# Twenty sums of weights staged in DRAM by the mixer, and a fourth seven-product pair in each later gate-and-up block of the last feed-forward part

## The chip, the cores and the metric

The kernel runs on one core of a Trainium2 chip. It has five engines that work at once and meet at semaphores: TensorE (PE, matrix products), VectorE (DVE), ScalarE (ACT), GpSimd (POOL) and SyncE (SP, which here only starts transfers). DMA engines, 16 of them for the core, move data between DRAM and the core's memory. The metric is the device time of one execution, in microseconds (us); lower is better.

## The reference

One decoder layer on 256 tokens of width 2048, all in float32: x + 0.5 FFN1, then a mixer (sliding-window attention beside an RWKV-7 recurrence, both gated), then cross-attention into a memory of 256 rows, then x + 0.5 FFN2, then a norm. What the change touches is the second feed-forward part; the mixer and the cross-attention matter as the time in which something else can be prepared.

```
def swiglu(h, w_gate, w_up, w_down):
    return (jax.nn.silu(h @ w_gate) * (h @ w_up)) @ w_down

x = x + 0.5 * swiglu(rms_norm(x, ffn1_norm), ffn1_w_gate, ffn1_w_up, ffn1_w_down)
x = gated_parallel_mixer(x, ...)        # w_in, attention, RWKV-7, w_proj_attn, w_proj_rwkv, w_out
x = memory_cross_attention(x, mem, ...) # w_q, w_kv, w_o
x = x + 0.5 * swiglu(rms_norm(x, ffn2_norm), ffn2_w_gate, ffn2_w_up, ffn2_w_down)
return rms_norm(x, final_norm)
```

w_gate and w_up are 2048 x 5632, w_down is 5632 x 2048. All weights are read from DRAM once.

## The kernel before

**Products of two parts.** PE multiplies numbers of reduced precision here, so every float32 operand is split into a high and a low part, and one product is three matmuls (`times`, L412 high by high, L413 with the weight's low part, L414 with x's low part). A matmul takes 128 rows of a weight and 512 columns for 128 tokens.

**Items.** Weights come in items of two blocks of 128 rows by 512 columns (0.524 MB; 512 KB). `weight_plan` lists them in the order of use: FFN1 is items 0 to 139, the mixer and the cross-attention 140 to 379 (W_in up to 299, projR 300 to 315, W_out 316 to 347, the cross-attention's from 348), FFN2 from 380 on. Of gate and up, both weights of a column block are taken together: such an item is a pair, two blocks of rows of gate and two of up, and a column block of 512 is eight pairs, numbered 0 to 7. There are eleven column blocks; the first (j = 0) is taken weight by weight.

**Splitting.** `load` (L331) has SP fetch an item, single ones four ahead, in 0.524 MB or, in the feed-forward parts, 1.05 MB for two items of the same weight. `divide` splits it one or two items ahead of PE: ACT rounds the raw weight to its high part (`hi`, L339) and DVE subtracts to get the low part (`lo`, L340). Raw tiles have four buffers, high and low parts three. So the load four items on waits for the subtraction that frees its buffer, and ACT's rounding waits until PE is done with the item three back. SP issues its transfers in the order of the program: what waits at the head of its queue holds everything behind it. There are eight counters for SP's transfers, used in turn, so a transfer also waits for the one eight before it.

**Seven products for eight.** A pair needs eight products: two row blocks, gate and up, two halves of the tokens. `product_pair` does it with seven where `SEVEN` names the pair (0, 2 and 4): products of sums of x (`combinations`) with sums of the four weight blocks. For such a pair `divide` forms four sums of weights with DVE (L366 to L369, 128x512 each), two tiles of them, and splits these too (`two_parts`, `thi` on ACT at L347, `tlo` on DVE at L348; each of the four tiles `thia`, `tloa`, `thib`, `tlob` has one buffer). Of the up weight then only one block is split. A plain pair is 24 matmuls on PE, a seven-product pair 21.

**Order.** Side work (norms, attention, the recurrence's steps, the memory's preparation) is written as coroutines in groups; `Interleave.tick`, called twice an item by `product`, lets each group go on by a step. The order of every engine's instructions is fixed thereby when the program is built. The recurrence runs from 1107 to 1272 us of the span; its products alternate with items of W_in on PE, its masks are written by DVE (`mk`, L1186) and its operands are fetched by POOL (`xb`, `rb`, L1150 and L1152). POOL also fetches x (L1351) and the memory (L1343) for the cross-attention.

**Memory.** In the mixer, work tiles of 128x4x256 float32 come from one ring, `t4`, of `N4` = 20 buffers.

```
def two_parts(v, e):
    sp = at["pool"]
    hi = sp.tile([P, KU, 512], F32R, tag="thi" + e, name="thi")
    lo = sp.tile([P, KU, 512], F32R, tag="tlo" + e, name="tlo")
    act.copy(hi[:], v[:])
    dve.tensor_tensor(lo[:], v[:], f32(hi[:]), ALU.subtract)
    return hi, lo
```

Of the kernel before, what the change touches and what calls it, by code (L numbers as in the profile page):

```python
# [7 lines left out]
F32 = mybir.dt.float32  # L8
F32R = mybir.dt.float32r
AF = mybir.ActivationFunctionType  # L10
ALU = mybir.AluOpType
# [4 lines left out]
P = 128  # L16
# [3 lines left out]
KD = D // P  # L20
# [7 lines left out]
KU = 2  # L28
# [1 line left out]

UP, DOWN = 2.0**40, 2.0**-40
GROUPS = ((0, 4), (4, 4), (8, 3))
N4 = 20

AHEAD, LOADED = 2, 4


SEVEN, SEVEN_DOWN = (0, 2, 4), ((2, 4, 6), (2, 4))


class Act:
# [39 lines left out]
def feed_forward_plan(wg, wu, wd, last):  # L81
    for j0, nj in GROUPS:
        for j in range(j0, j0 + nj):
            if j == 0:
                for w in (wg, wu):
                    yield w, 0, KD, 0, 512
            else:
                yield (wg, wu), 0, KD, (j * 512, j * 512), SEVEN
        yield (wd, wd), 4 * j0, 4 * nj, (0, 512), SEVEN_DOWN[nj < 4]
        if last and (j0, nj) == GROUPS[-1]:  # L90
            for n in (2, 3):
                yield wd, 4 * j0, 4 * nj, n * 512, 512
        else:
            yield (wd, wd), 4 * j0, 4 * nj, (1024, 1536), SEVEN_DOWN[1]
# [38 lines left out]
def decoder_layer(ctx: ExitStack, tc: tile.TileContext, a: dict, out: bass.AP):  # L133
    nc = tc.nc
# [13 lines left out]
    bg.group("chain", 3)  # L148
    bg.group("norm", 1)
    bg.group("mem", 1)  # L150

    def f32(x):
        return x.bitcast(F32)
# [14 lines left out]
    def idle(n):  # L168
        for _ in range(n):
            yield  # L170
# [9 lines left out]
    def select(out, in_, pattern, op, fill, base, mult):  # L180
        pool.affine_select(
            out=out, in_=in_, pattern=pattern, compare_op=op, fill=fill, base=base,
            channel_multiplier=mult,
        )

    ident = cpool.tile([P, P], F32, name="ident")
    select(ident[:], ones[:], [[-1, P]], ALU.is_equal, 0.0, 0, 1)
    bdup = cpool.tile([P, 2, P], F32, name="bdup")[:, 0, :]
    center = cpool.tile([P, P], F32, name="center")

    def mixer_constants(sp):

        abias = sp.tile([P, 2, P], F32, name="abias")
        pool.memset(abias[:], 0.0)
        select(abias[:, 0, :], abias[:, 0, :], [[1, P]], ALU.is_gt, NEG, 0, -1)
        select(abias[:, 1, :], abias[:, 1, :], [[-1, P]], ALU.is_ge, NEG, 0, 1)

        ups = sp.tile([P, 2, P], F32, name="ups")[:, 0, :]
        pool.memset(ups, UP)
        mask3 = sp.tile([P, 3, P], F32, name="mask3")  # L200
        select(mask3[:, 0, :], ups, [[1, P]], ALU.is_gt, 0.0, 0, -1)
        select(mask3[:, 1, :], ups, [[1, P]], ALU.is_ge, 0.0, 0, -1)
        select(mask3[:, 2, :], ups, [[1, P]], ALU.is_ge, 0.0, 0, -1)

        mask_l = sp.tile([P, P], F32, name="mask_l")
        select(mask_l[:], ups, [[-1, P]], ALU.is_gt, 0.0, 0, 1)
        bdones = sp.tile([P, P], F32, name="bdones")
        bdmean = sp.tile([P, P], F32, name="bdmean")
        pool.memset(bdones[:], 0.0)
        pool.memset(bdmean[:], 0.0)  # L210
        pool.memset(bdup, 0.0)
        for e in range(2):
            q = slice(64 * e, 64 * e + 64)
            pool.memset(bdones[q, q], 1.0)
            pool.memset(bdmean[q, q], 1.0 / 64)
            pool.memset(bdup[q, q], UP)
        pool.tensor_tensor(center[:], ident[:], bdmean[:], ALU.subtract)
        keep = sp.tile([P, 2, P], F32, name="keep")
        pool.memset(keep[:], 1.0)
        pool.memset(keep[:, :, 0:1], 0.0)  # L220
        return abias, mask3, mask_l, bdones, bdmean, keep

    sinks = cpool.tile([P, 16], F32, name="sinks")

# [69 lines left out]

    plan, units, items, ends = [], [], [], []
    for entry in weight_plan(a):
        if entry is None:
            ends.append(len(units))  # L300
            continue
        plan.append(entry)
        w, k0, nk, c0, n = entry
        if not isinstance(w, tuple):
            for k in range(k0, k0 + nk, KU):
                items.append(((len(units),), False))
                units.append((w, k, c0, n))
            continue
        for k in range(k0, k0 + nk, 2 * KU):
            u = len(units)  # L310
            units += [(v, k + i, c, 512) for v, c in zip(w, c0) for i in (0, KU)]
            items += [((u + i, u + 2 + i), (k - k0) // KU + i in n) for i in range(2)]
    raws, parts = {}, {}
    at = {"item": 0, "product": 0, "pool": None}

    def load(u, pieces=None):

        if u >= len(units) or u in raws:
            return
        w, k, c0, n = units[u]  # L320
        wide = at["pool"] is not None and (u < ends[0] or u >= ends[1] + LOADED)
        m = 2 if wide else 1
        if wide:
            raw = at["pool"].tile([P, m * KU, n], F32, tag="raw2", name="raw2", bufs=4)
        else:
            raw = wp.tile([P, KU, n], F32, tag="raw", name="raw", bufs=4)
        for i in range(m):
            raws[u + i] = raw[:, i * KU : (i + 1) * KU, :]
        for i, queue in pieces or ((slice(0, m * KU), nc.sync),):
            rows = slice((k + i.start) * P, (k + i.stop) * P)  # L330
            queue.dma_start(raw[:, i], w[rows, c0 : c0 + n].rearrange("(a p) n -> p a n", p=P))  # L331

    def split_unit(u, rows=slice(0, KU)):
        n, raw = units[u][3], raws[u]
# [16 lines left out]
    def divide(i):  # L351


        if i >= len(items) or i in parts:
            return
        which, seven = items[i]
        if len(which) == 1:
            parts[i] = split_unit(*which)
            return
        g, u = which  # L360
        if not seven:
            parts[i] = split_unit(g), split_unit(u)
            return
        rg, ru = raws[g], raws[u]
        t = [wp.tile([P, KU, 512], F32, tag="raw", name="raw", bufs=4) for _ in range(2)]
        dve.tensor_tensor(t[1][:, 0], ru[:, 0], rg[:, 0], ALU.subtract)  # L366
        dve.tensor_tensor(t[0][:, 0], ru[:, 1], ru[:, 0], ALU.subtract)
        dve.tensor_tensor(t[0][:, 1], ru[:, 1], t[1][:, 0], ALU.subtract)  # L368
        dve.tensor_tensor(t[1][:, 1], rg[:, 1], t[0][:, 1], ALU.subtract)  # L369
        a_ = two_parts(t[0], "a")  # L370
        parts[i] = split_unit(g), split_unit(u, slice(1, 2)), (a_, two_parts(t[1], "b"))

    def next_item():
        i = at["item"]
        at["item"] += 1
        u = items[i][0][0]
        for v in range(u, u + (2 * LOADED if at["pool"] is not None else LOADED)):
            load(v)
        divide(i)
        room = AHEAD  # L380
        for j in range(i + 1, min(i + 1 + AHEAD, len(items))):
            room -= len(items[j][0])
            if room < 0:
                break
            for v in items[j][0]:
                load(v)
            divide(j)
        return parts[i]

    def product(x: Act, w, skew=False):  # L390
# [30 lines left out]
                k + i == 0, k + i == nk - 1,  # L421
            )

    def combinations(sp, x: Act, seven, name, ready=lambda: True, early=True):

        pairs = [q for q in range(max(seven) + 1) if early or q in seven]
        n = 12 if not early else sum(4 if q in seven else 2 for q in pairs)
        parts = [sp.tile([P, n, P], F32R, tag=name + e, name=name + e) for e in ("hi", "lo")]  # L430
        c = {"parts": parts, "at": {}, "done": False, "seven": seven, "early": early}

# [220 lines left out]
    def feed_forward(sp, x, norm: Norm, wg, wu, wd, done, begin_last=lambda: None, last=False):  # L653
        if last:
# [6 lines left out]
                sp.tile(shape, dt, tag=tag, name=tag, bufs=bufs)  # L661
        begun = at["item"]
        c = combinations(
            sp, norm.x, SEVEN, "c", lambda: norm.r is not None and at["item"] > begun + 4
        )
        c["next"] = []
        for gi, (j0, nj) in enumerate(GROUPS):
# [1 line left out]
                [sp.tile([P, 16, T], F32R, tag="hhi", name="hhi")],  # L669
                [sp.tile([P, 16, T], F32R, tag="hlo", name="hlo")], 16,  # L670
            )
            ch = combinations(sp, h, SEVEN_DOWN[nj < 4], "d", early=False)

            def transposed(hb, c):
                for q in range(2):
# [90 lines left out]

    with tc.tile_pool(name="mx", bufs=1, reuse_waits="tile") as sp:
        aligned(sp)
        abias, mask3, mask_l, bdones, bdmean, keep = mixer_constants(sp)

        def t4(name, shape=(P, 4, T), dt=F32):
            return sp.tile(list(shape), dt, tag="t4", name=name, bufs=N4)

        def act_tiles(name, n):
            return Act(
# [386 lines left out]
        def pair(h, j):  # L1162
# [12 lines left out]
            for c in range(2):  # L1175
# [34 lines left out]
                def stage(lhs, rhs, o, first, name):  # L1210
                    for e, r in enumerate(rows):
                        pe.matmul(  # L1212
                            vb[:, o : o + P][:, r], lhs(e), rhs[:, r],
                            start=first and e == 0, stop=True, **ek,
                        )
                    s = small(name)
                    act.copy(s[:], vb[:, o : o + P])
                    return s
# [27 lines left out]
                if c == 0:  # L1246
                    s0 = small("s0")
                    dve.scalar_tensor_tensor(
                        s0[:], bs, dec[h][:, j : j + 1], bdup, ALU.mult, ALU.mult
                    )  # L1250
                yield
            bg.seen.add(f"y{4 * h + j}")
# [260 lines left out]
```

## Time and profile before

| | |
|---|---|
| time, median of 3 runs | 2262.58 us (2262.24 to 2262.78) |
| the profiled execution | 2263.34 us, of it 2261.6 in the span |
| TensorE's granted clock | 0.999 |
| busy: PE, DVE, ACT, POOL | 2246.8, 1778.4, 1226.9, 132.2 us |
| matmuls | 10617 records |
| moved by DMA | 432.49 MB, of it 13.11 MB written to DRAM; mean 191 GB/s |
| DVE, the four sums of a pair (L366 and the three after it), 128x512 | 687 ns each |
| ACT high part, 128x1024 and 128x512 | 1051 and 620 ns |
| DVE low part, 128x1024 and 128x512 | 1231 and 686 ns |
| ACT `thi`, DVE `tlo`, 172 of each | 1050 and 1220 ns |
| stages of the span | FFN1 to about 640 us, mixer and cross-attention to about 1560, FFN2 to the end |

A row of a stretch gives its length and the busy time of each engine with the count of instructions, then TensorE's clock as a share of full speed, the mean busy share of the 16 DMA engines (waiting transfers can make it pass 1) and the rate in GB/s. A timeline row gives start, duration, engine, line, operation, the tiles written and read, and in brackets the idle time before it with what ended it. Durations of PE's matmuls overlap; their starts do not. A row of the transfers gives the tile, the issuing queue, the count, the size and the time from issue to landing.

### The profile page before, as it was taken

To read this page: it belongs to the slowest core of one execution; us is meant where nothing else is said; L and a number is where in the kernel's file an instruction comes from. 1 tells how busy PE (TensorE), PEld (TensorE's weight loads), DVE (VectorE), ACT (ScalarE), POOL (GpSimd) and SP (SyncE) were. 2 spreads that over 40 slices of the span, in tenths; PEclk is the share of its full clock that TensorE was granted. 3 is DMA by queue.
4 is the path that set the end of the run, shared out by engine and by line. 5 is a ranking of instruction groups with operands and counts; after the bars stand their busy time and mean duration, and the time that the engine had idled before them with its cause. 6 is when DMAs were issued, how large, how long until landed. Compare 5 with 4: busy or idle time off the path is not lost.

```text
span 2261.6 us, 28110 instructions
## 1 busy us (share of the span) xinstructions
PE 2246.8 (99%) x10617; PEld 1845.5 (82%) x10617; DVE 1778.4 (79%) x2281; ACT 1226.9 (54%) x1653; POOL 132.2 (6%) x192
## 2 busy tenths in 40 slices
PE   9999999999999999999999999999999999999998
PEld 7888888888888877788888888888888888888886
DVE  7899989998988477886434566547899988998987
ACT  6555555555556477444435446456555455555554
POOL 1000000000001000301220030001000000000002
PEclk9999999999999999999999999999999999999999
DMA  7555565555556544666433476647555565555564
GB/s 262 186 206 199 190 210 199 186 204 205 189 200 200 161 135 155 216 214 208 147 90 100 143 257 218 203 166 271 187 203 201 191 211 198 186 205 205 186 209 145
DMA packets 219144, 432.49 MB, mean 191 GB/s; under 512 B 14108, under 2 KB 16385, under 8 KB 219009
## 3 DMA queue, kind: packets, MB, share of 16 engines
q1 hardware_dynamic: 210432, 404.78, 52.7%
q0 software_dynamic: 8112, 25.12, 3.5%
q8 instruction: 83, 1.36, 0.2%
q10 hardware_dynamic: 464, 0.79, 0.1%
q14 instruction: 53, 0.43, 0.1%
HBM read 417.56 MB, written 13.11 MB: 190 GB/s over the span
## 4 chain that ended last, share of the span: by engine, by line
PE 96%; DVE 2%; issue 1%; DMA 1%; ACT 1%; SPq 0%; POOL 0%; POOLq 0%; DVEq 0%; ACTq 0%
PE acc L412 19%; PE acc L413 19%; PE acc L414 19%; PE mm L414 8%; PE mm L412 8%; PE mm L413 8%; PE tr L600 2%; PE tr L413 2%; PE tr L412 2%; PE tr L414 2%; PE mm L1212 1%; PE tr L1181 1%; DVE lo L340 1%; DMA raw<-in_w_out_dram 0%; PE mm L827 0%
## 5 line engine op out<-in xcount | busy, mean ns | idle before, releaser
L340 DVE TENSOR_TENSOR lo<-raw,hi 128x1024 fp32r<-128x1024 f32 (+1 forms) x770 | 894.0, 1163 | 352.9 <-ACT hi L339 351.2
L339 ACT CAST hi<-raw 128x1024 fp32r<-128x1024 f32 (+1 forms) x770 | 759.7, 997 | 747.5 <-PE acc L414 528.5
L412 PE MATMUL acc<-hi,xhi 128*128 128x512 f32 (+1 forms) x1196 | 477.7, 400 | 2.1 <-ACT xhi L627 1.7
L413 PE MATMUL acc<-lo,xhi 128*128 128x512 f32 (+1 forms) x1196 | 465.7, 389 | 0.0
L414 PE MATMUL acc<-hi,xlo 128*128 128x512 f32 (+1 forms) x1196 | 465.0, 389 | 0.0
L412 PEld LDWEIGHTS acc<-hi,xhi 128*128 128x128 f32 x1196 | 225.3, 188 | 52.1 <-issue 5.5
L413 PEld LDWEIGHTS acc<-lo,xhi 128*128 128x128 f32 x1196 | 225.2, 188 | 45.8 <-issue 3.2
L414 PEld LDWEIGHTS acc<-hi,xlo 128*128 128x128 f32 x1196 | 224.6, 188 | 46.5 <-DVE xlo L628 1.0
L347 ACT CAST thi<-raw 128x1024 fp32r<-128x1024 f32 x172 | 178.9, 1050 | 57.6 <-DVE raw L368 44.2
L348 DVE TENSOR_TENSOR tlo<-raw,thi 128x1024 fp32r<-128x1024 f32 x172 | 208.3, 1220 | 0.7 <-ACT thi L347 0.4
L412 PE MATMUL mm<-hi,xhi 128*128 128x512 f32 x380 | 149.5, 393 | 0.0
L414 PE MATMUL mm<-hi,xlo 128*128 128x512 f32 x380 | 148.3, 390 | 0.0
L413 PE MATMUL mm<-lo,xhi 128*128 128x512 f32 x380 | 148.3, 390 | 0.0
L413 PE MATMUL acc<-lo,hhi 128*128 128x512 f32 x372 | 145.7, 392 | 0.8 <-DVE lo L340 0.8
L414 PE MATMUL acc<-hi,hlo 128*128 128x512 f32 x372 | 145.7, 392 | 0.0
L412 PE MATMUL acc<-hi,hhi 128*128 128x512 f32 x372 | 145.1, 390 | 0.0
L414 PEld LDWEIGHTS mm<-hi,xlo 128*128 128x128 f32 x380 | 71.4, 188 | 15.0
L413 PEld LDWEIGHTS mm<-lo,xhi 128*128 128x128 f32 x380 | 71.4, 188 | 14.4
L412 PEld LDWEIGHTS mm<-hi,xhi 128*128 128x128 f32 x380 | 71.5, 188 | 14.4
L413 PEld LDWEIGHTS acc<-lo,hhi 128*128 128x128 f32 x372 | 69.9, 188 | 15.4 <-DVE lo L340 1.2
L412 PEld LDWEIGHTS acc<-hi,hhi 128*128 128x128 f32 x372 | 69.9, 188 | 14.3
L414 PEld LDWEIGHTS acc<-hi,hlo 128*128 128x128 f32 x372 | 70.0, 188 | 13.9
(384 smaller groups left out, 3550.2 us busy)
## 6 DMA issues: line engine op xcount, KB each, us to landing
raw<-in_ffn_w_up_dram SPq DMA_DIRECT2D x88, 1024.0 KB, 5.3
raw<-in_ffn_w_down_dram SPq DMA_DIRECT2D x88, 1024.0 KB, 5.1
raw<-in_ffn_w_gate_dram SPq DMA_DIRECT2D x84, 1024.0 KB, 5.1
raw<-in_w_in_dram SPq DMA_DIRECT2D x136, 512.0 KB, 3.5
raw<-in_w_out_dram SPq DMA_DIRECT2D x32, 512.0 KB, 4.4
raw<-in_w_proj_attn_dram SPq DMA_DIRECT2D x16, 512.0 KB, 3.8
raw<-in_w_proj_rwkv_dram SPq DMA_DIRECT2D x16, 512.0 KB, 5.9
raw<-in_w_cross_kv_dram SPq DMA_DIRECT2D x16, 512.0 KB, 3.7
```

What stands on the lines that cost most here:

```text
L339: at["hi"] = act.copy(hi[:, s], raw[:, s])
L340: at["lo"] = dve.tensor_tensor(lo[:, s], raw[:, s], f32(hi[:, s]), ALU.subtract)
L347: act.copy(hi[:], v[:])
L348: dve.tensor_tensor(lo[:], v[:], f32(hi[:]), ALU.subtract)
L412: pe.matmul(o, xh, hi, start=first, stop=False, **how)
L413: pe.matmul(o, xh, lo, start=False, stop=False, **how)
L414: pe.matmul(o, xl, hi, start=False, stop=last, **how)
L600: pe.transpose(b[:, o : o + P], tok[:, t, col : col + P], ident[:])
L1181: pe.matmul(b[e][:, m * P : (m + 1) * P], x1[r, j, cs_], x2[r, j, cs_], start=True, stop=True,)
L1212: pe.matmul(vb[:, o : o + P][:, r], lhs(e), rhs[:, r], start=first and e == 0, stop=True, **ek,)
```

## The change

In FFN2, pairs 0, 1, 2 and 4 of each of the ten later column blocks take seven products (`SEVEN_2`), where 0, 2 and 4 did; FFN1 is as before. For pairs 1 and 2 (`STAGED`), 20 in all, the four sums of weights are not formed when the pair is reached. Twenty coroutines of a new last group do that during the mixer: each waits for an item (`STAGE_AT`: 253, 255 ... 271, then 310, 315 ... 355), has SP load the pair's gate and up blocks (two transfers of 0.524 MB) into two `t4` tiles, lets four ticks pass, forms the sums on DVE in two steps of two subtractions, each placed behind the latest low part, lets eight ticks pass and has SP store both tiles to a DRAM tensor `sums` (two transfers of 0.524 MB).

In FFN2, `load_sums` has SP fetch a pair's two tiles of sums into the ring of raw tiles, an item ahead, and `divide` takes these. The block of up rows that such a pair no longer uses (the sums hold it) is left out of the load of up; where pairs 1 and 2 lie in different loads of two, a load is cut in two pieces or shortened.

`combinations` of x makes the four sums for pair 1 too, so its tiles have 18 slots in FFN2. For the staging tiles the ring `t4` has 22 buffers; two constants, `bdup` and `center`, move from the constant pool into the mixer's.

By count of the built instructions: PE 30 matmuls fewer; ACT 20 roundings more; DVE 80 subtractions more in the mixer and in FFN2 40 subtractions fewer, 20 low parts more and three operations on x more; SP 130 transfers more (40 loads and 40 stores in the mixer, 40 loads of sums and 10 pieces more in FFN2).

```diff
-N4 = 20
+N4 = 22
...
 SEVEN, SEVEN_DOWN = (0, 2, 4), ((2, 4, 6), (2, 4))
+SEVEN_2, STAGED = (0, 1, 2, 4), (1, 2)
+
+
+STAGE_AT = [*range(253, 277, 2)][:10] + [*range(310, 370, 5)][:10]
...
-                yield (wg, wu), 0, KD, (j * 512, j * 512), SEVEN
+                yield (wg, wu), 0, KD, (j * 512, j * 512), SEVEN_2 if last else SEVEN
...
     bg.group("mem", 1)
+    bg.group("stage", 4)
...
-    bdup = cpool.tile([P, 2, P], F32, name="bdup")[:, 0, :]
-    center = cpool.tile([P, P], F32, name="center")
+    cpool.tile([P, P], F32, name="shift")
...
+        bdup = sp.tile([P, P], F32, name="bdup")
+        center = sp.tile([P, P], F32, name="center")
...
-            items += [((u + i, u + 2 + i), (k - k0) // KU + i in n) for i in range(2)]
-    raws, parts = {}, {}
+            for i in range(2):
+                q = (k - k0) // KU + i
+                if n == SEVEN_2 and q in STAGED:
+                    staged[len(items)] = len(staged)
+                items.append(((u + i, u + 2 + i), q in n))
+    raws, parts, summed = {}, {}, {}
+    first_unused = {items[i][0][1] for i in staged}
+    sums_d = dram.tile([len(staged), P, 4, 512], F32, name="sums")
...
+        if u in first_unused:
+            second = u + 1 in first_unused
+            pieces = [(slice(1, 2), nc.sync)] + [(slice(2 + second, 4), nc.sync)]
+            if not second:
+                pieces = ((slice(1, 4), nc.sync),)
+        elif u + 1 in first_unused and wide:
+            pieces = ((slice(0, 2), nc.sync), (slice(3, 4), nc.sync))
         for i, queue in pieces or ((slice(0, m * KU), nc.sync),):
             rows = slice((k + i.start) * P, (k + i.stop) * P)
             queue.dma_start(raw[:, i], w[rows, c0 : c0 + n].rearrange("(a p) n -> p a n", p=P))
+
+    def load_sums(i):
+
+        if i not in staged or i in summed:
+            return
+        summed[i] = [
+            wp.tile([P, KU, 512], F32, tag="raw", name="raw", bufs=4) for _ in range(2)
+        ]
+        for e, t in enumerate(summed[i]):
+            nc.sync.dma_start(t[:], sums_d[staged[i], :, KU * e : KU * e + KU, :])
+
+    def stage(t4, i, n):
+
+
+        while at["item"] < STAGE_AT[n]:
+            yield
+        t = t4("su", (P, KU, 512)), t4("sg", (P, KU, 512))
+        for e, v in zip(t, items[i][0][::-1]):
+            w, k, c0, _ = units[v]
+            rows = slice(k * P, (k + KU) * P)
+            nc.sync.dma_start(e[:], w[rows, c0 : c0 + 512].rearrange("(a p) n -> p a n", p=P))
+        yield from idle(4)
+        u0, u1, g0, g1 = (e[:, c] for e in t for c in range(KU))
+        with tc.issue_after(at["lo"].ins):
+            dve.tensor_tensor(g0, u0, g0, ALU.subtract)
+            dve.tensor_tensor(u0, u1, u0, ALU.subtract)
+        yield
+        with tc.issue_after(at["lo"].ins):
+            dve.tensor_tensor(u1, u1, g0, ALU.subtract)
+            dve.tensor_tensor(g1, g1, u1, ALU.subtract)
+        yield from idle(8)
+        for c, e in enumerate(t):
+            nc.sync.dma_start(sums_d[n, :, KU * c : KU * c + KU, :], e[:])
...
-        rg, ru = raws[g], raws[u]
-        t = [wp.tile([P, KU, 512], F32, tag="raw", name="raw", bufs=4) for _ in range(2)]
-        dve.tensor_tensor(t[1][:, 0], ru[:, 0], rg[:, 0], ALU.subtract)
-        dve.tensor_tensor(t[0][:, 0], ru[:, 1], ru[:, 0], ALU.subtract)
-        dve.tensor_tensor(t[0][:, 1], ru[:, 1], t[1][:, 0], ALU.subtract)
-        dve.tensor_tensor(t[1][:, 1], rg[:, 1], t[0][:, 1], ALU.subtract)
+        t = summed.get(i)
+        if t is None:
+            rg, ru = raws[g], raws[u]
+            t = [wp.tile([P, KU, 512], F32, tag="raw", name="raw", bufs=4) for _ in range(2)]
+            dve.tensor_tensor(t[1][:, 0], ru[:, 0], rg[:, 0], ALU.subtract)
...
             for v in items[j][0]:
                 load(v)
+            load_sums(j)
             divide(j)
+        load_sums(i + 2)
         return parts[i]
...
         c = combinations(
-            sp, norm.x, SEVEN, "c", lambda: norm.r is not None and at["item"] > begun + 4
+            sp, norm.x, SEVEN_2 if last else SEVEN, "c", lambda: norm.r is not None and at["item"] > begun + 4
         )
...
-            ch = combinations(sp, h, SEVEN_DOWN[nj < 4], "d", early=False)
+            ch = combinations(sp, h, SEVEN_DOWN[nj < 4], "d", early=False, n=12)
...
+        for i, n in staged.items():
+            bg.spawn("stage", stage(t4, i, n))
```

More of the change, by code (lines that the diff above doesn't have):

```diff
@@ L210, in mixer_constants @@
         pool.memset(bdmean[:], 0.0)
-        pool.memset(bdup, 0.0)
+        pool.memset(bdup[:], 0.0)
         for e in range(2):
@@ L220, in mixer_constants @@
         pool.memset(keep[:, :, 0:1], 0.0)
-        return abias, mask3, mask_l, bdones, bdmean, keep
+        return abias, mask3, mask_l, bdup, center, bdones, bdmean, keep
     sinks = cpool.tile([P, 16], F32, name="sinks")
@@ L292, in decoder_layer @@
     junk_t = cpool.tile([P, 512], mybir.dt.bfloat16, name="junk")
-    plan, units, items, ends = [], [], [], []
+    plan, units, items, ends, staged = [], [], [], [], {}
     for entry in weight_plan(a):
@@ L363, in divide @@
             return
-        rg, ru = raws[g], raws[u]
-        t = [wp.tile([P, KU, 512], F32, tag="raw", name="raw", bufs=4) for _ in range(2)]
-        dve.tensor_tensor(t[1][:, 0], ru[:, 0], rg[:, 0], ALU.subtract)
-        dve.tensor_tensor(t[0][:, 0], ru[:, 1], ru[:, 0], ALU.subtract)
-        dve.tensor_tensor(t[0][:, 1], ru[:, 1], t[1][:, 0], ALU.subtract)
-        dve.tensor_tensor(t[1][:, 1], rg[:, 1], t[0][:, 1], ALU.subtract)
+        t = summed.get(i)
[3 more added lines that the diff above has]
+            dve.tensor_tensor(t[1][:, 0], ru[:, 0], rg[:, 0], ALU.subtract)
+            dve.tensor_tensor(t[0][:, 0], ru[:, 1], ru[:, 0], ALU.subtract)
+            dve.tensor_tensor(t[0][:, 1], ru[:, 1], t[1][:, 0], ALU.subtract)
+            dve.tensor_tensor(t[1][:, 1], rg[:, 1], t[0][:, 1], ALU.subtract)
         a_ = two_parts(t[0], "a")
@@ L422, in multiply, with combinations @@
             )
-    def combinations(sp, x: Act, seven, name, ready=lambda: True, early=True):
+    def combinations(sp, x: Act, seven, name, ready=lambda: True, early=True, n=0):
         pairs = [q for q in range(max(seven) + 1) if early or q in seven]
-        n = 12 if not early else sum(4 if q in seven else 2 for q in pairs)
+        n = n or sum(4 if q in seven else 2 for q in pairs)
         parts = [sp.tile([P, n, P], F32R, tag=name + e, name=name + e) for e in ("hi", "lo")]
@@ L768, in decoder_layer @@
         aligned(sp)
-        abias, mask3, mask_l, bdones, bdmean, keep = mixer_constants(sp)
+        abias, mask3, mask_l, bdup, center, bdones, bdmean, keep = mixer_constants(sp)
         def t4(name, shape=(P, 4, T), dt=F32):
             return sp.tile(list(shape), dt, tag="t4", name=name, bufs=N4)
+        for i, n in staged.items():
+            bg.spawn("stage", stage(t4, i, n))
         def act_tiles(name, n):
@@ L1248, in pair @@
                     dve.scalar_tensor_tensor(
-                        s0[:], bs, dec[h][:, j : j + 1], bdup, ALU.mult, ALU.mult
+                        s0[:], bs, dec[h][:, j : j + 1], bdup[:], ALU.mult, ALU.mult
                     )
```

## The prediction

> **What bounds the kernel now.** I read the page's busy shares and chain first, then issue intervals in the timeline, then stretches of the span with their transfer rate, then waits and transfer latencies where the change adds work.
>
> ```profile
> span 2261.6 us, 28110 instructions
> PE 2246.8 (99%) x10617; PEld 1845.5 (82%) x10617; DVE 1778.4 (79%) x2281; ACT 1226.9 (54%) x1653; POOL 132.2 (6%) x192
> PE 96%; DVE 2%; issue 1%; DMA 1%; ACT 1%; SPq 0%; POOL 0%; POOLq 0%; DVEq 0%; ACTq 0%
> ```
>
> PE is idle for 14.8 us of the span: a matmul less is time won, and whatever makes PE wait is time lost. The row duration of a matmul (0.39 us) overlaps its neighbours; the price is the issue interval. PE's timeline, start then duration:
>
> ```profile
> 699.70 0.39 PE L412 MATMUL acc<-hi,hhi 128*128 128x512 f32 x1
> ...
> 704.46 0.39 PE L412 MATMUL acc<-hi,hhi 128*128 128x512 f32 x1
> ```
>
> 21 intervals lie between these starts: 4.76/21 = 0.2267 us each.
>
> Stretches: us, then busy PE, PEld, DVE, ACT, POOL, the clock, the DMA share, GB/s. First late FFN2 (lines 1 and 2), then where sums are to be staged, then the highest rate.
>
> ```profile
> 1800.00:1850.00 50.00, 50.00 (x222) 41.46 (x221) 44.26 (x53) 26.58 (x30) 0.00 (x0) 1.00 0.59 207
> 2000.00:2050.00 50.00, 50.00 (x222) 41.45 (x221) 47.26 (x59) 26.33 (x28) 0.00 (x0) 1.00 0.60 210
> 1080.00:1100.00 20.00, 20.00 (x100) 16.49 (x99) 12.41 (x17) 9.83 (x12) 8.48 (x12) 1.00 0.55 171
> 1335.00:1434.00 99.00, 98.73 (x472) 81.17 (x471) 62.85 (x79) 56.70 (x95) 13.43 (x13) 1.00 0.67 227
> 1357.00:1360.00 3.00, 3.00 (x17) 2.50 (x16) 1.56 (x2) 1.64 (x2) 1.48 (x3) 1.00 0.95 229
> 1369.00:1372.00 3.00, 3.00 (x15) 2.46 (x15) 0.27 (x2) 1.05 (x1) 0.00 (x0) 1.00 1.03 375
> 1550.00:1555.00 5.00, 5.00 (x27) 4.12 (x26) 3.81 (x6) 4.30 (x10) 1.45 (x2) 1.00 1.05 406
> ```
>
> FFN2 is PE's alone, with DVE close behind. From 1357 to 1372 us the DMA engines are full already. Why, and what it does to a weight load, is in the issues (KB, us to landing; stretches 1351 to 1354 and 1359 to 1362), POOL's timeline, and ACT's (a bracket is idle time and releaser):
>
> ```profile
> raw<-in_w_out_dram SPq DMA_DIRECT2D x1, 512.0 KB, 3.5
> raw<-in_w_out_dram SPq DMA_DIRECT2D x1, 512.0 KB, 11.0
> 1355.59 0.72 POOL L1351 DMA_DIRECT2D x<-x1d  x1
> 1356.31 2.17 POOL L1343 DMA_DIRECT2D mem<-in_mem_dram  x3
> 1361.33 0.72 POOL L1343 DMA_DIRECT2D mem<-in_mem_dram  x1 [2.85 <-PE tr L600]
> 1370.65 1.05 ACT L339 CAST hi<-raw 128x1024 fp32r<-128x1024 f32 x1 [2.91 <-DMA raw<-in_w_out_dram]
> 1374.45 1.05 ACT L339 CAST hi<-raw 128x1024 fp32r<-128x1024 f32 x1 [0.66 <-PE acc L414]
> ```
>
> Five POOL loads of 0.524 MB meet the loads of W_out; a load that took 3.5 us takes 11.0. The cast at 1370.65 is of item 324 (W_out's ninth). Its low part ends at 1372.97; PE begins the item when ACT may write the cast two items on, at 1374.45. So 1.5 us of cushion is left, and PE lost nothing.
>
> **The change, part by part.**
>
> *Fewer products.* Ten blocks of the last FFN have a fourth pair with seven products for eight: per block 3 matmuls fewer, 30 in all, each 128x512. 30 x 0.2267 = 6.8 us, in a stretch with no PE idle. All of it counts.
>
> *Splitting in FFN2.* Per block (41.5 us of PE before, 40.8 after) two pairs read staged sums. DVE is 44.26/50 to 47.26/50 busy, 36.7 to 39.2 us a block. The sums of pairs 0, 2 and 4 were 12 subtractions of 0.687; now only pairs 0 and 4 make them, 8 (-2.7); the fourth pair adds two low parts of 1.22 (+2.4) and halves one of 1.23 to 0.69 (-0.5): 35.9 to 38.4. ACT, 22 us, adds two casts of 1.05 and halves one to 0.62 (+1.7). Both stay under PE's 40.8. DMA: 2.1 MB of sums more and 0.5 MB of unused rows less per block, about 207 to 250 GB/s against 406. Free in sum. In order it is tighter: pairs 0, 1, 2 now follow each other and share one buffer each for the parts of their sums, and a subtraction for pair 4, which waits for a load, stands on DVE ahead of pair 2's last low part (slack about 0.4 us by the order of the rows). Before, such subtractions waited 9 times for 8.6 us in FFN2. Ends: below nothing (DVE has 0.8 us a block less) by perhaps 0.3, and 0.5 us in each of ten blocks, 5. I take 0.6: two blocks of ten (9 waits in 42) at 0.3 each.
>
> *Staging, first ten (items 253 to 275, 1063 to 1170 us).* Each adds 2.75 us to DVE (4 x 0.687) and 2.1 MB: two loads, two stores, all on SP between the weight loads. From the first of them to the load of item 266 stand 28 transfers of 0.524 MB, 14.7 MB in 41 us: 355 GB/s, where 171 to 185 ran. At the 385 that the full stretches keep, the loads land in time; at 350 my queue count has item 266 2.5 to 3 us late. DVE is 39 to 44 of 45 us full up to 1107, and in the recurrence subtractions stand ahead of masks (L1186) for which PE waits already (twice, 0.2 us). POOL's loads of the recurrence's operands wait for earlier stores, with some 6 us to spare. Ends 0 and 3 (no gain: nothing is removed here); I take 0.8, nearer to the 385.
>
> *Staging, second ten (items 310 to 358, 1324 to 1480 us).* 2.1 MB per five items (13.6 us) is 154 GB/s on top of 227: 381. Between bursts the backlog clears. In the burst at 1357 it does not: ahead of item 324's load SP now issues both stores of the 12th sum and both loads of the 13th, 2.1 MB at 385 = 5.4 us. One of POOL's memory loads goes out of the burst, since it now waits for a store of the 14th sum: -1.4; cushion -1.5. That leaves 2.5. The first store also waits on SP for its subtractions with item 323's load behind it (up to 2 us, part of it hidden), and the burst's own mean was 315 GB/s, by which 2.1 MB take 6.7. I take 3.3. [...] The memory load that now goes late has 5 to 9 us before PE transposes it; x's loads queued behind it on POOL have as much.
>
> [...]
>
> *Constants moved, one more buffer pair, x's combinations in 18 slots for 16.* No instruction on PE; DVE and ACT gain 3 and one wider operation in FFN2's first block, under 2 us beside 40.8 of PE. Nothing.
>
> **Sum.** -6.8 + 0.6 + 0.8 + 3.3 = -2.1. The profiled execution took 2263.34 (span 2261.6 and 1.7 around it), so 2261.2; it lies 0.76 above the median 2262.58, from which the forecast is 2260.5.
>
> **The rivals.**
> 1. *The transfers are absorbed.* For: 406 GB/s at 1550, 385 over 9 us of the burst, no PE loss before. Against: 1.5 us of cushion. With 0 to 2.3 us given back in all: 2255.8 to 2258.1, named 2257.
> 2. *Staged traffic is slower than weight loads, and PE waits (slower).* Place: the second ten. The trace has hardly any writes (13 of 432 MB) and the burst with mixed transfers averaged 315 GB/s. From item 307's load to the last store 54.5 MB go in 153 us, 356 GB/s; at 315 they take 173, 20 late, less some 10 of load-ahead: 10, and 3 in the first ten. 2262.6 - 6.8 + 13.6 = 2269.4. It decides once all waits pass 11.3 us (about 325 GB/s).
> 3. *Three seven-product pairs in a row make PE wait in every block of FFN2.* 0.3 to 0.5 us x 10 for the 0.6 above: 2263 to 2265, named 2263.5. For: one buffer per part; against: DVE and ACT keep 2.4 and 17 us a block to spare.
>
> **How the numbers follow.** 0.2% is 4.5 us, about what a measurement of this kernel tells from no change. Forecast (give-back 2.3 to 7) 0.36, of which 0.02 under -0.2%; rival 1 0.29; rival 2 0.23, of which 0.21 over +0.2%; rival 3 0.12, of which 0.03 over. Faster 0.31, same 0.45, slower 0.24. The range: from 2255.8 (all hidden) to 2269 (rival 2's middle), leaving out about 0.04 below and 0.12 above. The likeliest case alone: 2258.1 to 2262.8.
>
> **What will show it.** PE's matmuls 30 fewer and FFN2 6 to 7 us shorter with no wait over 1 us: first step right; waits of PE on tlo or lo (L413's kind) in FFN2: rival 3. Between 1360 and 1380 casts waiting for W_out's loads by 5 us and more, PE idle 2 to 5 us: the second ten as forecast; none: rival 1; PE idle in several stretches from 1340 to 1480: rival 2. The first ten: PE's wait around item 266 and on the masks. The forecast is wrong if the rate of loads and stores together differs much from 385, or if the recurrence's chain suffers more than the 0.8.

## The result, and the profile after

The changed kernel takes 2267.04 us (median of 12 runs, 2265.0 to 2269.73), the kernel before 2262.36 (12 runs, 2262.13 to 2262.79): a ratio of 1.0021, 95% interval 1.0013 to 1.0028. It is slower by 4.7 us, 0.2%. Its runs scatter over 4.7 us where those of before lie within 0.7. The profiled execution took 2266.5 us, 2264.8 of it in the span, 3.2 more than before (whose profiled execution was 1.0 above its median).

The page of the changed kernel: span, busy engines, and a row of transfers (last number: us from issue to landing).

```profile
span 2264.8 us, 28418 instructions
PE 2242.4 (99%) x10587; PEld 1837.5 (81%) x10587; DVE 1825.7 (81%) x2344; ACT 1246.7 (55%) x1673; POOL 132.9 (6%) x192
raw<-in_w_out_dram SPq DMA_DIRECT2D x32, 512.0 KB, 7.0
```

The 30 matmuls are gone (10617 records to 10587) and PE is busy for 4.4 us less, yet idle for 7.6 us more (22.4 for 14.8). W_out's loads take 7.0 us, where they took 4.4.

Where it happens can be read off item by item. ACT casts every item's high part, two items ahead of PE, so the start of item k's cast after, less that of before, is how late PE's work is at that place, as long as the cast stands at the same place in ACT's order in both. From the timelines of ACT in the two profiled executions (us late):

| item | 256 | 274 | 313 | 319 | 328 | 341 | 356 | 383 |
|---|---|---|---|---|---|---|---|---|
| late | 0.0 | 0.8 | 0.5 | 0.9 | 6.7 | 8.6 | 10.2 | 10.2 |

The first ten sums cost 0.5 us and the second ten 9.7: 0.4 up to item 319, 5.8 in the burst up to 328, 1.9 around item 334, 1.6 around 348. FFN2 then gains: PE's last matmul starts at 2255.95 us for 2252.71, 3.2 late, so 7.0 us are won back there. That is the whole of the 6.8 forecast.

Stretches of the changed kernel (length, busy PE, PEld, DVE, ACT, POOL, clock, DMA share, GB/s):

```profile
1340.00:1440.00 100.00, 94.69 (x438) 76.24 (x437) 73.19 (x99) 52.76 (x88) 13.30 (x13) 0.98 0.91 318
1370.00:1375.00 5.00, 4.24 (x19) 3.13 (x18) 2.60 (x3) 1.05 (x1) 0.00 (x0) 1.00 1.04 404
1375.00:1380.00 5.00, 3.17 (x12) 1.75 (x10) 3.43 (x5) 3.14 (x3) 0.00 (x0) 1.00 1.05 388
1380.00:1385.00 5.00, 3.83 (x12) 2.97 (x13) 3.54 (x6) 0.95 (x2) 0.00 (x0) 0.66 1.02 371
```

PE loses 5.3 of the 100 us from 1340 on, 3.8 of them from 1370 to 1385, while the DMA engines move 371 to 404 GB/s. So the transfers are not slow; whose come first is what counts, and that the queue's order decides. That is in the timelines of SP and of DVE and ACT of the changed kernel, from the burst (start, duration, engine and line; in brackets the idle time before and what ended it):

```profile
1350.64 4.90 SPq L351 DMA_DIRECT2D raw<-in_w_out_dram  x3
1360.29 0.34 SPq L384 DMA_DIRECT2D sums<-su  x1
1361.42 0.37 SPq L351 DMA_DIRECT2D raw<-in_w_out_dram  x1
1361.89 0.51 SPq L372 DMA_DIRECT2D su<-in_ffn_w_up_dram  x1
1362.57 0.44 SPq L372 DMA_DIRECT2D sg<-in_ffn_w_gate_dram  x1
1363.12 0.51 SPq L384 DMA_DIRECT2D sums<-sg  x1
```

```profile
1358.12 0.69 DVE L376 TENSOR_TENSOR sg<-su,sg 128x512 f32<-128x512 f32 x1 [2.97 <-DMA sg<-in_ffn_w_gate_dram]
1359.57 0.69 DVE L380 TENSOR_TENSOR su<-su,sg 128x512 f32<-128x512 f32 x1
1371.09 1.05 ACT L392 CAST hi<-raw 128x1024 fp32r<-128x1024 f32 x1 [5.57 <-DMA raw<-in_w_out_dram]
1376.20 1.04 ACT L392 CAST hi<-raw 128x1024 fp32r<-128x1024 f32 x1 [4.06 <-DMA raw<-in_w_out_dram]
```

Read it backwards. The cast at 1371.09 is of item 323, and it waits for its load. That load goes out at 1361.42; before it went at 1356.80. Ahead of it in SP's queue stands the store of the 12th sum, which waits until 1360.29 for the third subtraction (1359.57 to 1360.26). The subtractions stand idle on DVE for 2.97 us because the sum's own raw weights land only at 1358.1. Behind item 323's load go three more staged transfers, and then item 324's load. So one late transfer of staged data passes to DVE's queue, from there to SP's, and from there to PE.

Of the kernel before, the loads of W_out that SP issues between 1355 and 1375 us, item 323's first (count, ns of an issue, first and last start):

```profile
L331 SPq DMA_DIRECT2D raw<-in_w_out_dram x6: 367/368/368, 1356.8 to 1373.0; - x6
```

### The profile page after: what moved, and what is told of

The parts are those of the page before. It is cut to its first block, busy times and chain, and to the rows that moved or that the text cites. A ratio compares the mean times of both kernels' runs of the same rounds, so it can differ in the third digit from the quotient of the medians.

```text
span 2264.8 us, 28418 instructions
## 1 busy us (share of the span) xinstructions
PE 2242.4 (99%) x10587; PEld 1837.5 (81%) x10587; DVE 1825.7 (81%) x2344; ACT 1246.7 (55%) x1673; POOL 132.9 (6%) x192
## 4 chain that ended last, share of the span: by engine, by line
PE 92%; DVE 3%; DMA 2%; issue 1%; ACT 1%; SPq 0%; POOL 0%; POOLq 0%; ACTq 0%; DVEq 0%
PE acc L469 18%; PE acc L471 18%; PE acc L470 18%; PE mm L471 8%; PE mm L470 8%; PE mm L469 8%; PE tr L657 2%; PE tr L470 2%; PE tr L469 2%; PE tr L471 2%; DMA raw<-in_w_out_dram 1%; DVE lo L393 1%; PE mm L1272 1%; PE tr L1241 1%; ACT hi L392 0%
## 5 line engine op out<-in xcount | busy, mean ns | idle before, releaser
L469 PE MATMUL acc<-hi,xhi 128*128 128x512 f32 (+1 forms) x1166 | 465.6, 400 | 2.7 <-ACT xhi L684 2.2
L470 PE MATMUL acc<-lo,xhi 128*128 128x512 f32 (+1 forms) x1166 | 453.4, 389 | 0.0
L471 PE MATMUL acc<-hi,xlo 128*128 128x512 f32 (+1 forms) x1166 | 453.3, 389 | 0.0
L469 PEld LDWEIGHTS acc<-hi,xhi 128*128 128x128 f32 x1166 | 219.4, 188 | 51.1 <-issue 5.4
L471 PEld LDWEIGHTS acc<-hi,xlo 128*128 128x128 f32 x1166 | 218.8, 188 | 45.8 <-DVE xlo L685 1.0
L470 PEld LDWEIGHTS acc<-lo,xhi 128*128 128x128 f32 x1166 | 219.3, 188 | 44.4 <-issue 2.9
L401 DVE TENSOR_TENSOR tlo<-raw,thi 128x1024 fp32r<-128x1024 f32 x192 | 232.7, 1221 | 3.5 <-ACT thi L400 0.4
L400 ACT CAST thi<-raw 128x1024 fp32r<-128x1024 f32 x192 | 200.2, 1051 | 62.8 <-DVE raw L423 38.0
```

The costliest lines, as they stand in the source:

```text
L469: pe.matmul(o, xh, hi, start=first, stop=False, **how)
L470: pe.matmul(o, xh, lo, start=False, stop=False, **how)
L471: pe.matmul(o, xl, hi, start=False, stop=last, **how)
```

## The experiments

The theory after the traces: weight loads of the second ten's stretch come late behind staged transfers, while neither the first ten nor FFN2 matters. Rivals: a cost per staged sum wherever it is made; traffic alone; FFN2 giving back a part. For each run I give the time and the items' lateness by place, from its profiled execution as above: first ten (item 250 to 313), burst (319 to 328), then 328 to 341 and 341 to 356; and FFN2 (start of PE's last matmul against that of before, less the lateness at 383).

| run | time, us | before, us | first | burst | 328-341 | 341-356 | FFN2 |
|---|---|---|---|---|---|---|---|
| the changed kernel | 2267.04 | 2262.36 | 0.5 | 5.8 | 1.9 | 1.6 | -7.0 |
| first ten only | 2260.7 | 2262.38 | 2.0 | 0.2 | 0.0 | 0.0 | |
| second ten only | 2269.24 | 2262.38 | -0.3 | 4.6 | 0.8 | 1.3 | |
| all 20 in the recurrence | 2258.61 | 2262.38 | 1.2 | -0.3 | 0.0 | 0.0 | -5.7 |
| staging only | 2275.0 | 2262.38 | 1.1 | 5.1 | 1.7 | 2.2 | |
| FFN2 only | 2256.75 | 2262.49 | -0.3 | 0.5 | 0.0 | 0.0 | -7.1 |
| late stores | 2262.02 | 2262.49 | 0.5 | 3.0 | -0.2 | 2.5 | -6.1 |
| burst free | 2262.33 | 2262.49 | 1.7 | -0.5 | 1.6 | 1.2 | -5.6 |
| staging only, no stores | 2268.48 | 2262.49 | 0.8 | 4.7 | 3.6 | 0.2 | |
| staging only, no subtractions | 2267.51 | 2262.4 | 0.9 | 3.5 | 0.0 | 0.3 | |
| late both | 2261.57 | 2262.4 | 0.6 | 1.8 | -0.1 | 2.1 | -6.3 |
| recurrence, from 263 | 2265.16 | 2262.4 | 9.4 | 0.7 | 0.0 | 0.0 | -6.4 |
| spread | 2259.23 | 2262.47 | 0.8 | 0.2 | 0.0 | 0.0 | -5.9 |

FFN2 is given where all 20 pairs take seven products. Half a microsecond means nothing here: the run with FFN2 only stages nothing and reads -0.3 and 0.5, and the three runs with the FFN2 of before come out at 0.0 to -0.4 there.

For late both, item 329 stands for 328. In that run ACT's order has item 328's cast ahead of the rows of the norm behind which it stands before, so that cast is only 0.9 us late, while items 327 and 329 are 2.4 and 2.7 late, and PE itself is 2.4 late there (ACT's first operation on the transposes of x, which waits for PE there, starts at 1379.31 us for 1376.89).

**Each ten alone, all in the recurrence, staging without its use**

```diff
-                yield (wg, wu), 0, KD, (j * 512, j * 512), SEVEN_2 if last else SEVEN
+                yield (wg, wu), 0, KD, (j * 512, j * 512), SEVEN_2 if last and j <= 5 else SEVEN
```

> Only the ten sums of the recurrence are staged (items 253 to 271); five of the ten later blocks of FFN2 take pairs 0, 1, 2 and 4 in seven products, the other five 0, 2 and 4 as before. In those other five blocks one product of pair 1 takes a sum of x where a difference belongs, so that part of the result is not the reference's; the work is the same. Theory (weight loads come late behind the second ten's transfers, the first ten cost 0.5 us): 15 matmuls fewer, -3.4 + 0.5, about 2259.5 us. Rival (every staged sum costs its 0.5 us wherever it is made, by its operations on DVE and its slots on SP): -3.4 + 5, about 2264.

```diff
-STAGE_AT = [*range(253, 277, 2)][:10] + [*range(310, 370, 5)][:10]
+STAGE_AT = [*range(310, 370, 5)][:10]
...
-                yield (wg, wu), 0, KD, (j * 512, j * 512), SEVEN_2 if last else SEVEN
+                yield (wg, wu), 0, KD, (j * 512, j * 512), SEVEN_2 if last and j > 5 else SEVEN
```

> Only the ten sums from item 310 on are staged, the other five blocks of FFN2 as before (with one sum of x for a difference in pair 1, as in the run with the first ten). Theory: -3.4 + 9.7, about 2268.7 us, PE idle around items 320 to 327, 334 and 348 as in the changed kernel. Rival: -3.4 + 5, about 2264.

```diff
-STAGE_AT = [*range(253, 277, 2)][:10] + [*range(310, 370, 5)][:10]
+STAGE_AT = [*range(253, 293, 2)]
```

> All 20 sums are staged from item 253 to 291, one every two items, so none lies beside projR, W_out and the cross-attention; before, the transfers ran at 66 to 109 GB/s from 1120 to 1280 us. Theory: -7.0 + 0.5 to 1.5, about 2256.5 us, faster than both kernels. Rival (a cost per sum): about 2267 again. A third way, the recurrence's masks wait on DVE for the subtractions: over 2259.

```diff
-                yield (wg, wu), 0, KD, (j * 512, j * 512), SEVEN_2 if last else SEVEN
+                yield (wg, wu), 0, KD, (j * 512, j * 512), SEVEN
...
-                if n == SEVEN_2 and q in STAGED:
+                if len(items) > 395 and n == SEVEN and q in STAGED:
...
-    first_unused = {items[i][0][1] for i in staged}
+    first_unused = set()
...
-        if i not in staged or i in summed:
-            return
+        return
...
```

> All 20 sums are staged as in the changed kernel, but FFN2 is that of before (pairs 0, 2 and 4, sums formed there, full loads); the stored sums are not read. Theory: the mixer loses 10.2 us and FFN2 gains nothing, about 2272.5 us. If FFN2 itself gave back a part of its 6.8 us, this is nearer to the changed kernel: with 3 us given back, 2270.

Measured: 2260.7 (ratio 0.9995, 0.9986 to 1.0004, so no clear gain), 2269.24 (1.0031, 1.0020 to 1.0042), 2258.61 (0.9984, 0.9974 to 0.9993) and 2275.0 (1.0056, 1.0041 to 1.0071). The halves differ by 8.5 us, and their changes, -1.7 and +6.9, add up to 5.2 beside the changed kernel's 4.7. A cost per sum wherever it is made is out: the same 20 sums, all staged in the recurrence, make a kernel 3.8 us faster than before. The stretches of that run show where its traffic went:

```profile
1120.00:1280.00 160.00, 159.94 (x1063) 133.28 (x1063) 100.13 (x137) 70.95 (x164) 21.32 (x34) 1.00 0.81 272
1340.00:1440.00 100.00, 99.90 (x475) 82.18 (x474) 62.96 (x79) 56.47 (x94) 13.42 (x13) 1.00 0.67 220
```

From 1120 to 1280 us 272 GB/s are moved with 0.06 us of PE idle; from 1340 on the transfers are as before, and PE idles 0.1 us. The first ten alone cost 2.0 us in their profile (the longest of that run's ten executions), where the other runs with the same ten have 0.5 to 1.1; a slower clock has a part in it (last section).

**FFN2 alone**

```diff
-            bg.spawn("stage", stage(t4, i, n))
+            pass
...
-            nc.sync.dma_start(t[:], sums_d[staged[i], :, KU * e : KU * e + KU, :])
+            r = (KU * e + 4 * staged[i]) % 16 * P
+            nc.sync.dma_start(t[:], W["ffn1_w_gate"][r : r + 2 * P, 0:512].rearrange("(a p) n -> p a n", p=P))
```

> FFN2 as in the changed kernel, but nothing is staged: the tiles of sums are loaded from other weights of the same size, so the result of FFN2 is not the reference's; transfers, splitting and products are there in full. If FFN2 gains all of its 30 matmuls: 2262.4 - 6.8, about 2255.6 us. If three seven-product pairs in a row give some back (the run with all sums in the recurrence gained 5.6 in FFN2 by its trace): 2257.

Measured: 2256.75 (0.9975, 0.9965 to 0.9985), 5.7 us below before; the profiled execution, the fastest of its runs, has the full 7.1 in FFN2. Over the runs with sums FFN2 gains 5.6 to 7.1. The spread run, at 5.9, shows where a part of the difference goes: PE's weight loads wait for `tlo`, as in a block with three seven-product pairs in a row, and PE's matmuls idle 0.6 us by it. The rest was not traced. Waits of PE's weight loads in FFN2, first of FFN2 alone, then of the spread run (us, times, longest):

```profile
PEld tr L471 <- DVE tlo L402: 1.4, 5, 0.4
```

```profile
PEld tr L470 <- DVE tlo L401: 2.4, 7, 0.7
PEld acc L470 <- DVE tlo L401: 0.8, 1, 0.8
```

**Late stores, and the burst left free**

```diff
-        yield from idle(8)
+        yield from idle(8 if n < 10 else 16)
```

> The second ten's stores are placed 16 ticks after their subtractions in place of 8, so that they no longer hold the weight loads behind them on SP while the subtractions wait for their data. Nothing else changes. If the hold on SP is what makes the second ten dear (in the changed kernel item 323's load went out at 1361.4 in place of 1356.9): some 3 to 4 us less, about 2263.5. If it is the traffic alone: 2266 to 2267.

```diff
-STAGE_AT = [*range(253, 277, 2)][:10] + [*range(310, 370, 5)][:10]
+STAGE_AT = [*range(253, 277, 2)] + [310, *range(325, 365, 5)][:8]
```

> The sums of items 315 and 320 (those whose transfers meet POOL's five loads at 1357 us) are staged at items 273 and 275 in the recurrence; the other eight of the second ten stay at 310 and from 325 on. If the burst is the place: the 5.7 us lost between items 319 and 327 go, the 1.8 at item 334 and 1.6 at 348 stay, about 2261.5. If each sum of the second ten costs its tenth of 9.7 wherever it stands: 2265.

Measured: 2262.02 (0.9997, 0.9988 to 1.0007) and 2262.33 (0.9998, 0.9989 to 1.0008), each 5 us under the changed kernel. The second did what was expected by place: no loss in the burst, 1.6 and 1.2 at the other two. The first did so only in part. The 12th sum's first store still stands ahead of item 323's load; its second went out of the burst, as SP's timeline of that run shows:

```profile
1359.52 0.34 SPq L384 DMA_DIRECT2D sums<-su  x1
1360.65 0.37 SPq L351 DMA_DIRECT2D raw<-in_w_out_dram  x1
...
1373.60 0.46 SPq L384 DMA_DIRECT2D sums<-sg  x1
```

The burst still cost 3.0 us, half of the 5.8.

**Stores left out, subtractions left out, both late**

On top of the kernel with staging only:

```diff
-        for c, e in enumerate(t):
+        for c, e in enumerate(t if n < 10 else ()):
             nc.sync.dma_start(sums_d[n, :, KU * c : KU * c + KU, :], e[:])
```

> To be set beside the run with staging only (2275.0; FFN2 of before, the sums not read): the second ten's stores are left out, their loads and subtractions stay. Half of the added traffic goes, and the hold of the stores on SP with it. If the traffic with the hold makes the loss: 2266, the second ten's 9.5 us nearly gone. If the subtractions on DVE ahead of low parts make it: 2272 to 2275.

```diff
         with tc.issue_after(at["lo"].ins):
-            dve.tensor_tensor(g0, u0, g0, ALU.subtract)
-            dve.tensor_tensor(u0, u1, u0, ALU.subtract)
+            if n < 10:
+                dve.tensor_tensor(g0, u0, g0, ALU.subtract)
+                dve.tensor_tensor(u0, u1, u0, ALU.subtract)
...
-            dve.tensor_tensor(u1, u1, g0, ALU.subtract)
-            dve.tensor_tensor(g1, g1, u1, ALU.subtract)
+            if n < 10:
+                dve.tensor_tensor(u1, u1, g0, ALU.subtract)
+                dve.tensor_tensor(g1, g1, u1, ALU.subtract)
```

> To be set beside the run with staging only (2275.0): the second ten's subtractions are left out, so raw weights are stored, not sums (they are not read). All transfers stay; DVE waits for none of them ahead of a low part, and a store waits only for its own load. If the waits that stand in the order of DVE and SP (subtractions ahead of low parts, stores ahead of weight loads) make a large part of the loss: 2268 to 2270. If the traffic makes it: 2272 to 2275.

And on the changed kernel:

```diff
-        yield from idle(4)
+        yield from idle(4 if n < 10 else 10)
...
-        yield from idle(8)
+        yield from idle(8 if n < 10 else 14)
```

> The changed kernel with the second ten's subtractions 10 ticks after their loads (4 before) and the stores 14 ticks after them (8 before): neither DVE nor SP should wait for the staged data, all traffic stays. If the holds are the loss: 2262.0 (late stores alone) goes on down to 2258 or 2259. If the rest is traffic in the burst: 2261 to 2262.

Measured: 2268.48 (scattered, 2267.2 to 2272.2; between the two expectations), 2267.51 (just under what was expected of the waits) and 2261.57 (0.9996, 0.9987 to 1.0006; as expected if the rest is traffic). Without the stores half of the second ten's traffic is gone and SP is not held, but the profiled execution, one of the longer ones of that scatter, still lost 4.7 us in the burst. There DVE holds the low part. DVE and ACT in that run:

```profile
1371.20 1.05 ACT L391 CAST hi<-raw 128x1024 fp32r<-128x1024 f32 x1 [3.17 <-DMA raw<-in_w_out_dram]
1374.03 0.69 DVE L375 TENSOR_TENSOR sg<-su,sg 128x512 f32<-128x512 f32 x1 [4.74 <-DMA sg<-in_ffn_w_gate_dram]
1376.10 1.22 DVE L392 TENSOR_TENSOR lo<-raw,hi 128x1024 fp32r<-128x1024 f32 x1
```

The cast ends at 1372.25, and its low part could follow at once. It starts at 1376.10, behind three subtractions whose data landed only at 1374.0: 3.8 us. Without the subtractions that hold is gone, and a store waits only for its own load (SP waited 12.6 us for these, 4 times): 7.5 us under staging only, 3.5 left in the burst. With both placed later, all traffic still in the stretch (327 GB/s from 1340 to 1480, 328 in the changed kernel), no group of SP's waits for the staged subtractions is over 5.1 us, where the largest was 13.5 (1050 to 1480 us), and the burst costs 1.8. What is left there can be seen in ACT's timeline and in a stretch of that run:

```profile
1373.80 1.05 ACT L392 CAST hi<-raw 128x1024 fp32r<-128x1024 f32 x1 [3.34 <-DMA raw<-in_w_out_dram]
1375.00:1380.00 5.00, 3.46 (x14) 2.23 (x15) 4.87 (x6) 2.57 (x3) 0.00 (x0) 1.00 0.96 350
```

The cast is of item 324. Its load goes out 0.8 us later than before the change (1360.35 for 1359.52) and takes 13.3 us to land, where it took 11.0. PE idles 1.5 us of the 5, then none from 1380 to 1455. So in the burst the two holds, with the slower clock that followed them, are about two thirds of the loss (5.8 down to 1.8): the one on SP by itself left 3.5 us, the one on DVE 4.7 (with a slower clock in it, last section). The remaining 1.8 is, by these rows, a weight load that lands late among the staged transfers. Item 334 costs nothing in this run, but 2.1 us stay around item 348, and the time came to 2261.57, not to the 2258 to 2259 that the holds alone predicted.

What makes the loss at the two later places was narrowed down, not taken apart. Without the subtractions, with every transfer kept, they cost 0.0 and 0.3 us, where staging only has 1.7 and 2.2. Yet the DMA engines are as full (stretches of the run without subtractions):

```profile
1405.00:1410.00 5.00, 5.00 (x28) 4.12 (x27) 3.78 (x6) 4.48 (x10) 0.00 (x0) 1.00 1.07 351
1455.00:1460.00 5.00, 5.00 (x24) 4.10 (x23) 2.91 (x5) 3.68 (x8) 0.00 (x0) 1.00 0.98 380
```

A full queue alone thus does not make the loss there; it takes the subtractions, or what waits for them. The changed kernel has one more suspect, on POOL (its timeline):

```profile
1402.30 0.72 POOL L1403 DMA_DIRECT2D mem<-in_mem_dram  x1 [39.59 <-DMA sums<-su]
```

The last load of the memory has moved 40 us on, since its tile was last used by the staging of the 14th sum, and meets a full stretch there (399 GB/s from 1405 to 1410). A stretch as full need not cost by itself: in the run without subtractions 389 GB/s are moved from 1400 to 1405 us, and PE is busy for all of the 5 us.

**Where in the recurrence**

```diff
-STAGE_AT = [*range(253, 277, 2)][:10] + [*range(310, 370, 5)][:10]
+STAGE_AT = [263 + 3 * i // 2 for i in range(20)]
```

> All 20 sums in the recurrence, but from item 263 to 291 (three sums every two or so of the slow items), clear of the stretch from 1063 to 1100 us that ran at 171 to 185 GB/s before the change and 347 to 380 in the changed kernel. If what the first ten cost (0.5 to 1.7) is traffic in that stretch: 2257.5, a microsecond under the run from 253 on (2258.6). If the subtractions hold the recurrence's chain: 2260 or more.

```diff
-STAGE_AT = [*range(253, 277, 2)][:10] + [*range(310, 370, 5)][:10]
+STAGE_AT = [*range(237, 273, 4)] + [*range(273, 295, 2)]
```

> All 20 sums staged ahead of projR, thinner at first: nine from item 237 to 269, one every four items (2.1 MB in 10.9 us, 193 GB/s on top of 183, below the 385 that the full stretches keep), eleven from 273 to 293, one every two slow items. If what is left in the run from 253 on (2258.6 us; 1.2 us late by item 313) is traffic and order in the dense stretch 1063 to 1114 us: 2257.3, near FFN2's part alone (2256.75). If a staged sum costs some 0.1 us wherever it is made, or the last ones run into projR: 2258.6 or more.

Measured: 2265.16 (1.0012, 1.0003 to 1.0021) and 2259.23 (0.9985, 0.9976 to 0.9994). The first is a miss with a plain reason. No more than four sums are under way at a time, each with its idle ticks, so the queue fell behind: the lateness is 0.2 us at item 292 and 11.5 at 304, where the last sums run into projR.

```profile
ACT hi L392 <- DMA raw<-in_w_proj_rwkv_dram: 13.3, 7, 5.7
```

The spread run is as fast as the one from 253 on (2258.61), not faster; the dense start was not what stayed over FFN2's 2256.75. Both beat the kernel before, and the changed kernel by 8 us.

## Why the prediction was wrong

The forecast was 2.1 us less; the medians show 4.7 more, the two profiled executions 3.2 more (-7.0 + 0.5 + 9.7). Nearly all of the difference is one term of the sum.

*Fewer products, -6.8, and splitting in FFN2, +0.6.* Right: FFN2 gained 7.0 in the changed kernel and 5.6 to 7.1 over the runs, with waits on `tlo` of the size I had put there. Rival 3 is out.

*Staging, first ten, +0.8.* Right: 0.5 in the profile, 0.5 to 2.0 over the runs.

*Staging, second ten, +3.3.* This step failed: 9.7. Of it, 5.8 is the burst that I had worked out, where I had 3.3. The transfers and the memory load that leaves the burst were as counted, and the full rate held (388 GB/s from 1357 to 1372 us, where I had taken 385). What I had sized too low is the hold. The bytes ahead of item 324's load gave 2.5 in my sum, and with both steps placed later the burst cost 1.8: that part was about right. For the holds and a lower rate the sum had the other 0.8; the holds cost 4.0, the slower clock that followed them included. With the holds nearly gone the second ten still cost 4.3 (item 313 to 383), 1.8 of it in the burst. I gave SP's wait for the first store "up to 2 us, part of it hidden", and the load of item 323 went out 4.6 us late. For the subtractions on DVE I had charged their duration, not their wait for data that lands late (2.97 us in the rows above). And I had no term for the clock (below), 1.7 us. The other 3.5 us fall at items 334 and 348, where I had written that between bursts the backlog clears. It does not: with a sum every five items the share of the DMA engines was 0.93 to 1.06 from 1400 to 1415 and from 1435 to 1465. That alone is not the cause, since the run without subtractions has shares as high and loses 0.0 and 0.3 there; what the subtractions hold at these two places stays open. The loads of the memory and of x, which I had moved there at no cost, came on top of the traffic; that they cost anything is not shown.

*Rival 2* named nearly the time (2269.4) for another reason, by luck: staged traffic at 315 GB/s. Its sign, PE idle in several stretches, came true, its mechanism did not. The rate was 371 to 404 GB/s while PE waited. The chip moved the bytes as fast as I took it to; they were the wrong bytes first.

## What to carry to other kernels

Work moved under a stage's cover was paid for in this burst mostly by the order of the queues (4.0 of 5.8 us, the slower clock included), which busy shares do not show: a step that waits for its own late data, at the head of an in-order queue (a subtraction on DVE, a store on SP), hands its lateness to the weights behind it (item 323's load went out 4.6 us late). So place each step where its data has long landed, and put the traffic where the rate is low: here 66 to 109 GB/s in the recurrence against stretches with bursts to 400 (DVE is also less busy there before the change, 65.8 of 160 us; the runs do not separate the two). The second was worth more here: 2258.61 us with all sums in the recurrence, 2261.57 with both steps later. And when buffers are shared, look at whose later load inherits the wait.

## What the runs showed of the hardware that I had not expected

After its stalls PE lost time once more. Its timeline in the changed kernel, after the burst:

```profile
1377.30 0.51 PE L469 MATMUL acc<-hi,mthi 128*128 128x512 f32 x1 [1.05 <-ACT hi L392]
1378.56 0.50 PE L470 MATMUL acc<-lo,mthi 128*128 128x512 f32 x1 [0.76 <-DVE lo L393]
...
1380.90 0.33 PE L657 MATMUL tr<-ident,x 128*128 128x128 f32 x1 [0.92 <-DVE x L1414]
...
1383.02 0.63 PE L471 MATMUL acc<-hi,mtlo 128*128 128x512 f32 x1
1383.45 0.63 PE L469 MATMUL acc<-hi,mthi 128*128 128x512 f32 x1
```

From about 1381.6 to 1385 us the granted clock is 0.50 (0.78 over the microsecond from 1381, 0.50 over the next two), and matmuls start every 0.43 us, not every 0.2267: 0.34 x 5 = 1.7 us lost with PE busy all the while, so that no wait and no idle time shows it. The same stands in the profiles of the runs with the second ten only, with staging only and, twice, with the stores left out (clock 0.66 to 0.77 over 5 us), but in none that lost 3.5 us or less in the burst. The run with the first ten alone has it too, from 1110 to 1115 us (0.66), where the changed kernel kept 1.00: about 1.7 us again, the whole difference between its 2.0 us and the 0.5 of the changed kernel, though PE idled as long there in both (0.67 us from 1105 to 1110). What sets the clock down is thus not told by the idle time alone. In the changed kernel PE was busy for 3.17 of 5 us from 1375 to 1380, for 0.1 from 1380 to 1381 and for 0.73 from 1381 to 1382; the run without subtractions had it busy for only 2.55 of 5 us from 1375 to 1380 and for 4.73 in the next five, and its clock stayed at 1.00 in both.
